# Values as the stationary operand in column halves, scores two pairs ahead, and the output half per token tile

## The chip, the core and the metric

The kernel runs on one core of a Trainium2 chip. What counts is the device time of one execution in microseconds, as the median over runs. TensorE is written PE (its weight loads PEld), VectorE DVE, ScalarE ACT, GpSimd POOL, SyncE SP.

## The reference, cut to what matters

All arithmetic is float32, one sequence of 256 tokens, width 1024. Two first-block layers hold a mixer, a cross attention to a memory of 256 rows, and a gated convolution network. Two second-block layers hold a gated network, a mixer and another gated network. The parts that the change touches are the attentions:

```python
# first mixer: 8 heads of neighbourhood attention (all 4 rows of keys are seen here,
# with a bias and a column mask) and 8 query heads over 2 key heads; head size 64
p = softmax(scores); o = p @ v
out = concat([na_out, gqa_out], -1) @ w_out
# memory block: 4 heads of size 128; second mixer: 16 heads of size 64, causal;
# and beside it the state-space part:
xdt   = silu(xs) * dt
cb    = C_chunk @ B_chunk.T
y     = (cb * lmat) @ xdt + carry(chunk 0 -> chunk 1) + d_skip * silu(xs)
```

## The kernel before, in words

Activations are held transposed, features on partitions, as two fp32r parts, high and low (`Features`), and every weight matrix product is three fp32r matmuls (`mm3`, L256). A weight unit of 128x2048 comes by two DMAs on SP's queue (`wunit`, L234); ACT copies it to `hi`, DVE subtracts to `lo`, with three buffers of each. Such a product costs 3 matmuls of 256 or 512 moving columns per feature tile.

Attention works in pairs of heads (`Pair`, L414) for one token tile of 128 queries. `S` multiplies queries (stationary) with keys; heads of size 64 lie in the two row halves of the array, and two pairs (mates) share one S step. On DVE and ACT `softmax` (L532) takes the row maximum, then exp with the row sum as a by-product (`den`). `T` transposes the unnormalised probabilities on PE (2 transposes of 128x128 per head with 256 keys) and ACT copies them to SBUF (`pts`). `V` multiplies: stationary the transposed probabilities (128 keys by 128 queries), moving the values of a head (64 columns; 128 in the memory block), so that a bank `po` collects [queries, 8 heads x 64]. All these are plain float32 matmuls, which stand as two records each in the trace; transposes stand as one. At the end of a group (8 heads, or 4 in the memory block) `divide` (L477) multiplies `po` by the reciprocal of `den` into SBUF, and `turn` (L484) transposes it back with four transposes; `split` (L401) writes the two parts of the result.

`pipeline` (L495) sets the order by hand: at step i it issues S of pair i+look, T of pair i, V of pair i-1, and `turn` two steps after a group's end; one step more and the group's key is in `done`. After each of these it yields, and `weave` (L161) issues filler steps at a rate. PE's order is exactly this order; for the other engines a planner orders by the text and by when operands are ready. In the first mixer the filler (L710) is `values()` (16 steps of one `mm3`), then, once token tile 1 of the grouped heads is done, `half_g()` (L691: the output projection of the grouped half, both token tiles, 16 steps), then the first quarter of `half_n()`. It starts with three steps owed at rate 1.0 and look=1. The memory block and the second mixer have look=2; the latter's filler is `conv()`.

`ssd()` (L1128) is the state-space part, woven with the projection of the gate. Its text: silu of xs, the two `xdt` products, `xd0` (chunk 0 times its decay), two `d_skip` products, four `cb` products with their masks, then eight rounds: `decay()` of the next round (L1149: DVE makes `ar`, PE sums it into `sg`, ACT takes exp, DVE multiplies by the masked `cb`), `across()` in rounds 0 and 1 (the carry between chunks, which needs `xd0` and `xs`), and the products `y`.

Of the kernel before, what the change touches and what calls it, by code (L numbers as in the profile page):

```python
# [16 lines left out]
P = 128  # L17
# [95 lines left out]
def unit(a, spec):  # L113

    kind, name, l, r0, c0 = spec
    if kind == "G":
        (ng, nv), (cg, cv) = name, c0
        both = np.stack([a[ng][l][:, cg : cg + P], a[nv][l][:, cv : cv + P]], 1)
        return both.reshape(KD, P, 2 * P).transpose(1, 0, 2).reshape(P, 2048)
    w = a[name][l]  # L120
    if kind == "T":
        z = np.zeros((P, 2048), w.dtype)
        z.reshape(P, 2, KD, P)[:, 0, :, :16] = w[:, c0 : c0 + 16].reshape(KD, P, 16).transpose(1, 0, 2)
        return z
    if kind == "W":
        return w[:, c0 : c0 + 256].reshape(8, P, 256).transpose(1, 0, 2).reshape(P, 2048)
    if kind == "M":
        return w[r0 : r0 + 512, c0 : c0 + 512].reshape(4, P, 512).transpose(1, 0, 2).reshape(P, 2048)
    return w[r0 : r0 + 256, :].reshape(2, P, 1024).transpose(1, 0, 2).reshape(P, 2048)

# [7 lines left out]
class Ring:  # L138


    N = {"w1": (8, 256), "w2": (7, 640), "rb": (2, 256)}

    def __init__(self, pool):
        self.pool = pool
# [31 lines left out]
def two_blocks(ctx: ExitStack, tc: tile.TileContext, specs, x, mem, wall, pf, rowb, fin, rpb, cst, out):  # L176
# [237 lines left out]
    class Pair:  # L414


        def __init__(self, hs, pos, st, nm, n, kts, scores, soft, v, vcol, w):
            self.__dict__.update(hs=hs, pos=pos, st=st, nm=nm, n=n, kts=kts, scores=scores, soft=soft, v=v, vcol=vcol, w=w, end=None, mate=None, beside=None)

        def S(self):  # L420
            n = self.n
            if self.mate is None:
                p = ps(f"s_{self.nm}")
                at = [p[:, b * n : (b + 1) * n] for b in range(2)]
                for b in range(2):
                    self.scores(at[b], b)
                self.pr = [self.soft(at[b], b) for b in range(2)]
            elif self.mate is not True:

                both = (self, self.mate)  # L430
                p = [ps(f"s{b}_{self.nm}") for b in range(2)]
                for j, x in enumerate(both):
                    for b in range(2):
                        x.scores(p[b][:, j * n : (j + 1) * n], b)
                for j, x in enumerate(both):
                    x.pr = [x.soft(p[b][:, j * n : (j + 1) * n], b) for b in range(2)]

        def T(self):
            p = ps(f"pt_{self.nm}")
# [7 lines left out]
        def V(self):  # L447
            st, w, n = self.st, self.w, self.n
            if "po" not in st:
                st["po"] = ps(f"po_{self.nm}")  # L450
            for b in range(2):
                o = st["po"][:, self.pos[b] * w : (self.pos[b] + 1) * w]
                for kt in range(self.kts):
                    T.matmul(o, self.pt[:, b * n + kt * P : b * n + (kt + 1) * P], self.v[:, kt, self.vcol(b) : self.vcol(b) + w],
                             start=kt == 0, stop=kt == self.kts - 1)

    def attention(nm, nheads, tts, mixT, base, group, keys, scores, soft, v, vcol, apart=1, fours=True):

# [2 lines left out]
        pairs = []  # L461
        for tt in tts:
            for g0 in range(0, nheads, group):
                st = {"den": sm.tile([P, 8], F32, tag="den", name=f"den_{nm}{tt}{g0}")}
                firsts = [i for i in range(group) if (i // apart) % 2 == 0]
                for n_, a in enumerate(firsts):
                    pos = (a, a + apart)
                    hs = (g0 + a, g0 + a + apart)
                    pairs.append(Pair(
                        hs, pos, st, f"{nm}{tt}_{g0 + a}", keys(tt), keys(tt) // P,  # L470
                        lambda o, b, hs=hs, tt=tt: scores(o, hs[b], tt),
                        lambda s, b, hs=hs, tt=tt, st=st, pos=pos: soft(s, hs[b], tt, st["den"][:, pos[b] : pos[b] + 1], f"{nm}{tt}_{hs[b]}"),
                        v, lambda b, hs=hs: vcol(hs[b]), w))
                    if fours and n_ % 2:
                        pairs[-2].mate, pairs[-1].mate = pairs[-1], True

                def divide(st=st, tt=tt, g0=g0):  # L477
                    rd = sm.tile([P, 8], F32, tag="rd", name=f"rd_{nm}{tt}{g0}")
                    V.reciprocal(rd[:, :group], st["den"][:, :group])
                    st["o"] = wk.tile([P, 512], F32, tag="w2", name=f"o_{nm}{tt}{g0}")  # L480
                    V.tensor_tensor(st["o"].rearrange("p (h d) -> p h d", h=group), st["po"].rearrange("p (h d) -> p h d", h=group),
                                    bl(rd[:, :group], w), ALU.mult)

                def turn(st=st, tt=tt, g0=g0):  # L484
                    p = ps(f"ot_{nm}{tt}{g0}")
                    for i in range(4):
                        T.transpose(p[:, i * P : (i + 1) * P], st["o"][:, i * P : (i + 1) * P], ident)
                    split(mixT.four(base + g0 * w // 512, tt), p.rearrange("p (a b) -> p a b", a=4))

                pairs[-1].end = (divide, turn, (nm, tt, g0))  # L490
        return pairs

    done = set()
# [1 line left out]
    def pipeline(pairs, look=1, before_v=None, drain=5, lag=2):  # L495
        pend = []
        n = len(pairs)
        for i in range(-look, n + 1):
# [10 lines left out]
            if i >= 1:  # L509
                pairs[i - 1].V()  # L510
                if pairs[i - 1].end:
                    pairs[i - 1].end[0]()
                    pend.append((i + lag, pairs[i - 1].end[1]))
                    pend.append((i + lag + 1, lambda k=pairs[i - 1].end[2]: done.add(k)))
                yield
            while pend and pend[0][0] <= i:
                pend.pop(0)[1]()
# [29 lines left out]
    def mixer1(l, nrm, nx):  # L547
# [140 lines left out]
                       lambda s, h, tt, den, nm: softmax(s, na_bias(h, tt), den, nm), nv, lambda h: h * 64)  # L688


        def half_g():  # L691
            for c in range(2):
                p = [ps(f"wg{l}{c}{tt}") for tt in range(2)]
                yield from gen_M("w_out", l, 512, c * 512, list(enumerate(p)), mixT, 4, 4)
                for tt in range(2):
                    residual(tt, c, p[tt])

        units = []

# [7 lines left out]
                    yield  # L707
            residual(tt, c, p)

        fill = chain(values(), after((f"gq{l}", 1, 0), half_g()), after((f"na{l}", 0, 0), half_n(0, 0)))  # L710
        weave(pipeline(gqa + na, drain=4), fill, 1.0, 3)
        run(fill)
        run(half_n(0, 1))
        run(half_n(1, 0))
# [196 lines left out]
    def mixer2(l, nrm, nx):  # L911
# [216 lines left out]
        def ssd():  # L1128
# [2 lines left out]
            late.pop(0)()  # L1131
            for tt in range(2):
                A.activation(xs[:, tt, :], xs[:, tt, :], AF.Silu)
            for tt in range(2):
                V.tensor_tensor(h16(xdt[:, tt, :]), h16(xs[:, tt, :]), bl(dt[:, tt * 16 : (tt + 1) * 16], 64), ALU.mult)
            V.tensor_tensor(h16(xd0), h16(xdt[:, 0, :]), bl(dec[:, 0:16], 64), ALU.mult)
            for tt in (1, 0):
                V.tensor_tensor(h16(xs[:, tt, :]), h16(xs[:, tt, :]), bl(rbc("d_skip_2", l), 64), ALU.mult)

            for g in range(4):  # L1140
                p = ps(f"cb{nm}{g}")
# [27 lines left out]

            todo = [(g, c) for g in range(4) for c in range(2)]  # L1170
            lms = {todo[0]: decay(*todo[0])}
            yield
            yp = {}
            for i, (g, c) in enumerate(todo):
                if i + 1 < len(todo):
                    lms[todo[i + 1]] = decay(*todo[i + 1])
                    yield
                if i < 2:
                    across(i)
                yield  # L1180
                q = g // 2
                if (c, q) not in yp:
# [136 lines left out]
```

## Time and profile before

| | us |
|---|---|
| median of 3 runs | 1973.94 |
| lowest and highest | 1973.42, 1974.88 |
| profiled execution | 1978.73 |
| its span (first to last instruction) | 1976.9 |
| mean granted PE clock in it | 0.993 |

The busy time of PE counts each matmul to its modelled end; matmuls overlap, so the busy time of a group is not the sum of what its members cost. What one costs in a stream is the distance from its start to the next start. The granted clock is 1.00 at 2.4 GHz and 0.50 at 1.2 GHz.

### The profile page before, as it was taken

Reading aid. Unit: us, or ns where it says so; the run is one execution under the profiler, and the core shown is the slowest. Engines: PE = TensorE matmul, PEld = TensorE weight load, DVE = VectorE, ACT = ScalarE, POOL = GpSimd, SP = SyncE. Lnnn points to the kernel's source line nnn. Section 1 sums busy time; section 2 is a strip of 40 time slices with the busy share of each in tenths; the row PEclk is TensorE's granted clock in tenths of the full one; section 3 lists DMA queues with packets and bytes.
Section 4 is the critical chain, followed back from the end, with each engine's and each line's share of the span. In section 5 each row is a group of like instructions: output and inputs, shape, how many; then the busy total and the mean of one; then the engine's idle time right before and its main releaser. Section 6 shows DMA issues by size and latency. Waiting matters only on the chain.

```text
span 1976.9 us, 33687 instructions
## 1 busy us (share of the span) xinstructions
PE 1954.4 (99%) x13082; PEld 1787.3 (90%) x13082; DVE 1405.1 (71%) x3065; ACT 1057.8 (54%) x1801; POOL 7.6 (0%) x108
## 2 busy tenths in 40 slices
PE   8999999999999999999999999999999999999999
PEld 7788999887999999999899789999999889889998
DVE  6666887775778778656868876666655868877564
ACT  5565555655665555444576554445444567555442
POOL 0000000000000000000000000000000000000000
PEclk9899999999999999999999999999999999999999
DMA  7334565552436555555543356555555553355553
GB/s 264 122 108 155 169 200 188 185 182 86 167 124 212 186 187 180 184 190 183 170 157 113 105 161 207 183 185 169 194 191 187 179 169 117 107 161 178 186 183 124
DMA packets 90992, 331.01 MB, mean 167 GB/s; under 512 B 10064, under 2 KB 10576, under 8 KB 90576
## 3 DMA queue, kind: packets, MB, share of 16 engines
q1 hardware_dynamic: 90832, 328.86, 50.6%
q8 instruction: 102, 1.67, 0.3%
q14 instruction: 58, 0.48, 0.1%
HBM read 327.77 MB, written 1.05 MB: 166 GB/s over the span
## 4 chain that ended last, share of the span: by engine, by line
PE 94%; DVE 3%; ACT 1%; DMA 1%; issue 1%; SPq 0%; DVEq 0%; ACTq 0%
PE upffn L259 26%; PE upc L259 13%; PE accffn L259 12%; PE accc L259 6%; PE xbb L259 5%; PE wob L259 4%; PE qkb L259 4%; PE vb L259 2%; PE zb L259 2%; PE gq L259 1%; PE wg L259 1%; PE mk L259 1%; PE mq L259 1%; DMA raw<-in_wall 1%; PE mo L259 1%; PE mv L259 1%
## 5 line engine op out<-in xcount | busy, mean ns | idle before, releaser
L253 DVE TENSOR_TENSOR lo<-raw,hi 128x512 fp32r<-128x512 f32 x1220 | 795.2, 685 | 223.7 <-ACT hi L250 222.2
L250 ACT ACTIVATE hi<-raw 128x1024 fp32r<-128x1024 f32 (+1 forms) x611 | 628.3, 1052 | 594.1 <-issue 365.9
L259 PE MATMUL upffn<-hT_s,hi 128*128 128x256 f32 x2816 | 509.5, 283 | 0.0
L259 PEld LDWEIGHTS upffn<-hT_s,hi 128*128 128x128 f32 x2816 | 441.7, 192 | 3.0
L259 PE MATMUL upffn<-hT_s,lo 128*128 128x256 f32 x1408 | 398.4, 283 | 0.0
L259 PEld LDWEIGHTS upffn<-hT_s,lo 128*128 128x128 f32 x1408 | 270.1, 192 | 0.0
L259 PE MATMUL upc<-hT_f,hi 128*128 128x256 f32 x1408 | 254.9, 283 | 0.0
L259 PE MATMUL accffn<-hi,mix_fffn 128*128 128x512 f32 x704 | 223.8, 390 | 0.0
L259 PEld LDWEIGHTS upc<-hT_f,hi 128*128 128x128 f32 x1408 | 220.9, 192 | 1.6
L259 PE MATMUL upc<-hT_f,lo 128*128 128x256 f32 x704 | 199.2, 283 | 0.0
L259 PEld LDWEIGHTS accffn<-hi,mix_fffn 128*128 128x128 f32 x704 | 132.3, 188 | 26.7
L901 DVE TENSOR_TENSOR u_ffn<-upffn,rb_s 128x512 f32<-128x512 f32 x80 | 55.2, 690 | 126.6 <-PE upffn L259 126.6
L259 PE MATMUL accffn<-lo,mix_fffn 128*128 128x512 f32 x352 | 137.4, 390 | 0.0
L259 PEld LDWEIGHTS upc<-hT_f,lo 128*128 128x128 f32 x704 | 135.0, 192 | 0.0
L259 PE MATMUL accc<-hi,mix_fc 128*128 128x512 f32 x352 | 112.1, 390 | 0.0
L259 PE MATMUL xbb<-hT_b,hi 128*128 128x256 f32 x512 | 103.3, 297 | 0.0
L259 PEld LDWEIGHTS xbb<-hT_b,hi 128*128 128x128 f32 x512 | 78.3, 190 | 3.6 <-issue 2.6
L259 PE MATMUL qkb<-hi,hT_b 128*128 128x512 f32 x256 | 81.0, 393 | 0.0
L259 PEld LDWEIGHTS accc<-hi,mix_fc 128*128 128x128 f32 x352 | 66.2, 188 | 13.3
L259 PEld LDWEIGHTS accffn<-lo,mix_fffn 128*128 128x128 f32 x352 | 66.2, 188 | 12.2
L259 PE MATMUL xbb<-hT_b,lo 128*128 128x256 f32 x256 | 72.1, 282 | 0.0
L259 PE MATMUL accc<-lo,mix_fc 128*128 128x512 f32 x176 | 68.7, 390 | 0.0
(403 smaller groups left out, 3001.6 us busy)
## 6 DMA issues: line engine op xcount, KB each, us to landing
raw<-in_wall SPq DMA_DIRECT2D x609, 512.0 KB, 4.2
TB<-in_rpb SPq DMA_DIRECT2D x2, 1536.0 KB, 9.5
MEM<-in_mem SPq DMA_DIRECT2D x2, 1024.0 KB, 4.9
x_in<-in_x SPq DMA_DIRECT2D x4, 256.0 KB, 5.5
out<-x_in SPq DMA_DIRECT2D x4, 256.0 KB, 2.0
C<-in_cst SPq DMA_DIRECT2D x1, 544.0 KB, 9.3
raw<-in_wall SPq DMA_DIRECT2D x2, 256.0 KB, 6.8
FIN<-in_fin SPq DMA_DIRECT2D x1, 512.0 KB, 7.6
```

Of the source, the lines that this page charges most:

```text
L250: A.activation(hi[:, q], raw[:, i : i + n], AF.Copy)
L253: V.tensor_tensor(lo[:, q], raw[:, i : i + LOW], hi[:, q].bitcast(F32), ALU.subtract)
L259: T.matmul(o, st[a], mv[b], start=first and i == 0, stop=last and i == 2)
L901: V.tensor_tensor(u, p, b2(rb), ALU.mult)
```

## The change

`V` swaps the operands: the values of a head are stationary (128 keys by 64 columns) and the transposed probabilities are moving (128 queries). The two heads of a pair write the two partition halves of `po`, that is the two column halves of the array, in turn over the key tiles. `po` so holds the transposed output; `turn` goes, and `split` reads `po` at once. Since the rows are now features, the division moves ahead of the transposes: after the softmax each pair gets a reciprocal and one multiplication per head on the probabilities, in SBUF. For the grouped heads (pairs of head a and a+4) the rows of `w_out` are laid out on the host to fit. The first mixer's pipeline looks two pairs ahead, its filler runs at rate 0.8 with nothing owed, and `half_g` runs per token tile, with its two weight units kept from the first token tile to the second. The ring of 256-wide work tiles has 14 buffers instead of 8. In `ssd()` only the first `xdt` product stands at the beginning; the second follows the first `decay()`, `xd0` and the first `d_skip` the second `decay()`, the other `d_skip` the third, and `across()` moves to rounds 2 and 4.

```diff
+        if name == "w_out" and r0 == 512:
+            w, r0 = w[512:].reshape(2, 4, 64, -1).transpose(1, 0, 2, 3).reshape(512, -1), 0
...
-    N = {"w1": (8, 256), "w2": (7, 640), "rb": (2, 256)}
+    N = {"w1": (14, 256), "w2": (7, 640), "rb": (2, 256)}
...
                 self.pr = [self.soft(at[b], b) for b in range(2)]
+                self.divide()
...
                     x.pr = [x.soft(p[b][:, j * n : (j + 1) * n], b) for b in range(2)]
+                    x.divide()
+        def divide(self):
+            rd = sm.tile([P, 2], F32, tag="rd", name=f"rd_{self.nm}", bufs=4)
+            V.reciprocal(rd, self.den)
+            for b in range(2):
+                V.tensor_scalar(self.pr[b][:, : self.n], self.pr[b][:, : self.n], rd[:, b : b + 1], None, ALU.mult)
...
-            for b in range(2):
-                o = st["po"][:, self.pos[b] * w : (self.pos[b] + 1) * w]
-                for kt in range(self.kts):
-                    T.matmul(o, self.pt[:, b * n + kt * P : b * n + (kt + 1) * P], self.v[:, kt, self.vcol(b) : self.vcol(b) + w],
-                             start=kt == 0, stop=kt == self.kts - 1)
+            both = [(b, kt) for b in range(2) for kt in range(self.kts)]
+            if w == 64:
+                both.sort(key=lambda x: x[1])
+            for b, kt in both:
+                r, c = (rows[b], self.at) if w == 64 else (slice(0, P), self.at + b)
+                T.matmul(st["po"][r, c * P : (c + 1) * P], self.v[:, kt, self.vcol(b) : self.vcol(b) + w],
+                         self.pt[:, b * n + kt * P : b * n + (kt + 1) * P], start=kt == 0, stop=kt == self.kts - 1)
...
-                def divide(st=st, tt=tt, g0=g0):
-                    rd = sm.tile([P, 8], F32, tag="rd", name=f"rd_{nm}{tt}{g0}")
-                    V.reciprocal(rd[:, :group], st["den"][:, :group])
-                    st["o"] = wk.tile([P, 512], F32, tag="w2", name=f"o_{nm}{tt}{g0}")
-                    V.tensor_tensor(st["o"].rearrange("p (h d) -> p h d", h=group), st["po"].rearrange("p (h d) -> p h d", h=group),
-                                    bl(rd[:, :group], w), ALU.mult)
-                def turn(st=st, tt=tt, g0=g0):
-                    p = ps(f"ot_{nm}{tt}{g0}")
-                    for i in range(4):
-                        T.transpose(p[:, i * P : (i + 1) * P], st["o"][:, i * P : (i + 1) * P], ident)
-                    split(mixT.four(base + g0 * w // 512, tt), p.rearrange("p (a b) -> p a b", a=4))
-                pairs[-1].end = (divide, turn, (nm, tt, g0))
+                def put(st=st, tt=tt, g0=g0):
+                    split(mixT.four(base + g0 * w // 512, tt), st["po"].rearrange("p (a b) -> p a b", a=4))
+                pairs[-1].end = (put, (nm, tt, g0))
...
-                    pend.append((i + lag, pairs[i - 1].end[1]))
-                    pend.append((i + lag + 1, lambda k=pairs[i - 1].end[2]: done.add(k)))
+                    pend.append((i + lag, lambda k=pairs[i - 1].end[1]: done.add(k)))
...
-        def half_g():
+        units_g = []
+        def half_g(tt):
             for c in range(2):
-                p = [ps(f"wg{l}{c}{tt}") for tt in range(2)]
-                yield from gen_M("w_out", l, 512, c * 512, list(enumerate(p)), mixT, 4, 4)
-                for tt in range(2):
-                    residual(tt, c, p[tt])
+                p = ps(f"wg{l}{c}{tt}")
+                if tt == 0:
+                    units_g.append(wunit("M", "w_out", l, 512, c * 512))
+                for k in range(4):
+                    mm3(p, mixT.k(4 + k, tt), cut(units_g[c], k * 512, (k + 1) * 512), k == 0, k == 3)
+                    yield
+                residual(tt, c, p)
...
-        fill = chain(values(), after((f"gq{l}", 1, 0), half_g()), after((f"na{l}", 0, 0), half_n(0, 0)))
-        weave(pipeline(gqa + na, drain=4), fill, 1.0, 3)
+        fill = chain(values(), after((f"gq{l}", 0, 0), half_g(0)), after((f"gq{l}", 1, 0), half_g(1)),
+                     after((f"na{l}", 0, 0), half_n(0, 0)))
+        weave(pipeline(gqa + na, 2, drain=4), fill, 0.8)
...
-            for tt in range(2):
+            def times_dt(tt):
                 V.tensor_tensor(h16(xdt[:, tt, :]), h16(xs[:, tt, :]), bl(dt[:, tt * 16 : (tt + 1) * 16], 64), ALU.mult)
-            V.tensor_tensor(h16(xd0), h16(xdt[:, 0, :]), bl(dec[:, 0:16], 64), ALU.mult)
-            for tt in (1, 0):
+            def times_d(tt):
                 V.tensor_tensor(h16(xs[:, tt, :]), h16(xs[:, tt, :]), bl(rbc("d_skip_2", l), 64), ALU.mult)
+            times_dt(0)
...
             lms = {todo[0]: decay(*todo[0])}
+            times_dt(1)
             yield
             yp = {}
             for i, (g, c) in enumerate(todo):
                 if i + 1 < len(todo):
                     lms[todo[i + 1]] = decay(*todo[i + 1])
                     yield
+                if i == 0:
+                    V.tensor_tensor(h16(xd0), h16(xdt[:, 0, :]), bl(dec[:, 0:16], 64), ALU.mult)
                 if i < 2:
-                    across(i)
+                    times_d(i)
+                if i in (2, 4):
+                    across(i // 2 - 1)
```

## Rows read from the trace of the kernel before

**Rows 1.** The page, part 1: busy us, share of the span, instructions.

```profile
PE 1954.4 (99%) x13082; PEld 1787.3 (90%) x13082; DVE 1405.1 (71%) x3065; ACT 1057.8 (54%) x1801; POOL 7.6 (0%) x108
```

**Rows 2.** Stretches of core 0: length, busy time by engine, granted clock, DMA.

```profile
75.09:100.12 25.03, 23.74 (x138) 19.38 (x136) 11.29 (x38) 15.30 (x44) 0.00 (x0) 0.73 0.15 45
442.83:463.85 21.02, 19.17 (x138) 15.35 (x136) 10.78 (x37) 14.02 (x40) 0.00 (x0) 0.92 0.17 51
1006.36:1079.76 73.40, 73.40 (x626) 70.47 (x625) 59.66 (x178) 53.23 (x126) 0.63 (x6) 1.00 0.35 113
1093.71:1103.66 9.95, 6.65 (x16) 5.05 (x16) 7.37 (x15) 4.39 (x7) 0.00 (x0) 0.66 0.16 53
1709.22:1718.07 8.85, 5.51 (x16) 4.07 (x16) 7.37 (x15) 4.39 (x7) 0.00 (x0) 0.81 0.19 60
```

**Rows 3.** Waits of TensorE: us in total, times, longest.

```profile
PE sgb L1154 <- DVE ar_b L1153: 6.6, 2, 3.3
```

**Rows 4.** Timeline of TensorE, first mixer: start, length to the modelled end, instructions.

```profile
69.80 1.13 PE L673 MATMUL s_gq<-G,qm 64*128 64x256 f32 x8
70.87 0.50 PE L259 MATMUL nav<-hi,hT_a 128*128 128x512 f32 x1
...
71.69 0.60 PE L443 MATMUL pt_gq<-C,pr_gq 128*128 128x128 f32 x4
72.04 0.48 PE L259 MATMUL nav<-hi,hT_a 128*128 128x512 f32 x1
...
72.82 1.00 PE L454 MATMUL po_gq<-G,pts_gq 128*128 128x64 f32 x8
73.64 0.48 PE L259 MATMUL nav<-hi,hT_a 128*128 128x512 f32 x1
```

**Rows 5.** Timeline of TensorE, ssd() of layer 0, full clock.

```profile
1105.26 0.62 PE L1154 MATMUL sgb<-ar_b,gtr 128*128 128x512 f32 x2
...
1108.66 1.00 PE L1186 MATMUL yb<-xdt_b,lm_b 128*128 128x64 f32 x8
```

**Rows 6.** Timeline of TensorE: second block's scores and products, memory block's products.

```profile
1011.06 0.40 PE L259 MATMUL xbb<-hT_b,hi 128*128 128x256 f32 x2
1011.30 0.28 PE L259 MATMUL xbb<-hT_b,lo 128*128 128x256 f32 x1
1011.51 0.71 PE L1020 MATMUL s_db<-kT_b,qm 64*128 64x128 f32 x8
1012.15 0.50 PE L259 MATMUL xbb<-hT_b,hi 128*128 128x256 f32 x2
...
1015.55 0.56 PE L454 MATMUL po_db<-v_b,pts_db 128*128 128x64 f32 x4
1015.92 0.48 PE L259 MATMUL xbb<-hT_b,hi 128*128 128x256 f32 x2
...
178.18 1.06 PE L454 MATMUL po_me<-M,pts_me 128*128 128x128 f32 x8
179.02 0.50 PE L259 MATMUL mo<-hi,mix_m 128*128 128x512 f32 x1
```

**Rows 7.** Groups of DVE by form: count, busy us, mean ns of one.

```profile
L481 DVE TENSOR_TENSOR o_db<-po_db,rd_db 128x512 f32<-128x512 f32 x8 | 5.5, 684 | 2.1 <-PE po_db L454 2.1
...
L345 DVE TENSOR_SCALAR dg_s<-C,y_s 128x128 f32<-128x128 f32 x8 | 1.9, 284 | 0.1
...
L479 DVE RECIPROCAL rd_me<-den_me 128x4 f32<-128x4 f32 x4 | 0.7, 168 | 0.0
```

**Rows 8.** Timeline of TensorE, first transposes of layer 0; idle time in brackets.

```profile
60.19 0.90 PE L443 MATMUL pt_gq<-C,pr_gq 128*128 128x128 f32 x4 [0.66 <-ACT pr_gq L539]
```

**Rows 9.** Timeline of DVE before the second decay().

```profile
1089.27 2.35 DVE L1135 TENSOR_TENSOR xdt_b<-xs_b,dt_b 128x1024 f32<-128x1024 f32 x2
1091.54 1.21 DVE L1136 TENSOR_TENSOR xs_b<-xdt_b,dec_b 128x1024 f32<-128x1024 f32 x1
1092.68 2.34 DVE L1138 TENSOR_TENSOR xs_b<-xs_b,RBt 128x1024 f32<-128x1024 f32 x2
```

More of the change, by code (lines that the diff above doesn't have):

```diff
@@ L414, in two_blocks, with __init__ @@
     class Pair:
-        def __init__(self, hs, pos, st, nm, n, kts, scores, soft, v, vcol, w):
-            self.__dict__.update(hs=hs, pos=pos, st=st, nm=nm, n=n, kts=kts, scores=scores, soft=soft, v=v, vcol=vcol, w=w, end=None, mate=None, beside=None)
+        def __init__(self, hs, at, st, nm, n, kts, scores, soft, v, vcol, w):
+            self.__dict__.update(hs=hs, at=at, st=st, nm=nm, n=n, kts=kts, scores=scores, soft=soft, v=v, vcol=vcol, w=w, end=None, mate=None, beside=None)
         def S(self):
@@ L463, in attention @@
             for g0 in range(0, nheads, group):
-                st = {"den": sm.tile([P, 8], F32, tag="den", name=f"den_{nm}{tt}{g0}")}
+                st = {}
                 firsts = [i for i in range(group) if (i // apart) % 2 == 0]
                 for n_, a in enumerate(firsts):
-                    pos = (a, a + apart)
                     hs = (g0 + a, g0 + a + apart)
+                    den = sm.tile([P, 2], F32, tag="den", name=f"den_{nm}{tt}{g0}{a}", bufs=4)
                     pairs.append(Pair(
-                        hs, pos, st, f"{nm}{tt}_{g0 + a}", keys(tt), keys(tt) // P,
+                        hs, n_ if w == 64 else a, st, f"{nm}{tt}_{g0 + a}", keys(tt), keys(tt) // P,
                         lambda o, b, hs=hs, tt=tt: scores(o, hs[b], tt),
-                        lambda s, b, hs=hs, tt=tt, st=st, pos=pos: soft(s, hs[b], tt, st["den"][:, pos[b] : pos[b] + 1], f"{nm}{tt}_{hs[b]}"),
+                        lambda s, b, hs=hs, tt=tt, den=den: soft(s, hs[b], tt, den[:, b : b + 1], f"{nm}{tt}_{hs[b]}"),
                         v, lambda b, hs=hs: vcol(hs[b]), w))
+                    pairs[-1].den = den
                     if fours and n_ % 2:
                         pairs[-2].mate, pairs[-1].mate = pairs[-1], True
-                def divide(st=st, tt=tt, g0=g0):
-                    rd = sm.tile([P, 8], F32, tag="rd", name=f"rd_{nm}{tt}{g0}")
-                    V.reciprocal(rd[:, :group], st["den"][:, :group])
-                    st["o"] = wk.tile([P, 512], F32, tag="w2", name=f"o_{nm}{tt}{g0}")
-                    V.tensor_tensor(st["o"].rearrange("p (h d) -> p h d", h=group), st["po"].rearrange("p (h d) -> p h d", h=group),
-                                    bl(rd[:, :group], w), ALU.mult)
-                def turn(st=st, tt=tt, g0=g0):
-                    p = ps(f"ot_{nm}{tt}{g0}")
-                    for i in range(4):
-                        T.transpose(p[:, i * P : (i + 1) * P], st["o"][:, i * P : (i + 1) * P], ident)
-                    split(mixT.four(base + g0 * w // 512, tt), p.rearrange("p (a b) -> p a b", a=4))
-                pairs[-1].end = (divide, turn, (nm, tt, g0))
+                def put(st=st, tt=tt, g0=g0):
+                    split(mixT.four(base + g0 * w // 512, tt), st["po"].rearrange("p (a b) -> p a b", a=4))
+                pairs[-1].end = (put, (nm, tt, g0))
         return pairs
```

## The prediction

> **What bounds the kernel now.** I read the page first: TensorE is busy 99% of the span [rows 1], so on the average there is nothing to fill. That average hides its own gaps, because the ends of matmuls are modelled and a matmul at the half clock counts as busy. So I went on to the busy time by stretches [rows 2], the waits of TensorE [rows 3] and the timeline, in which the distance from one start to the next start is the true price. There the reader is to see three places:
>
> 1. First block's mixer, from the last step of values() to the first of half_g(): no filler is left, and attention runs alone, for 25.03 us in layer 0 and 21.02 us in layer 1, with a mean granted clock of 0.73 and 0.92 [rows 2]. By the loop L495 a stretch holds 8 T, 8 V, 4 S and 2 turn() of 4 records, 8, 8 and 4: 32+64+32+8 = 136, against 138 in the row. At the prices among filler [rows 4], T 72.04-71.69 = 0.35, V 73.64-72.82 = 0.82, S 70.87-69.80 = 1.07, turn() like T: 2.80+6.56+4.28+0.70 = 14.34 us. So 10.69 and 6.68 us are lost, 17.4 in both layers, in waits on the chain S, max, exp, T, copy, V, and in the fall from the 2.4 to the 1.2 GHz level that follows.
> 2. Start of ssd(): TensorE waits 3.3 us per layer for ar, the input of the second decay() [rows 3], and then falls to 1.2 GHz. From the end of the matmul before the wait to the first y products 9.95 and 8.85 us pass [rows 2]; the same sequence of instructions takes 1108.66-1105.26 = 3.40 at full clock [rows 5]. Lost: 6.55+5.45 = 12.0 us.
> 3. Everywhere else around the change TensorE is dense: second block's attention, 73.40 us of layer 0, has TensorE busy throughout and DVE 59.66, 81% [rows 2].
>
> **The change part by part.**
>
> *Transposes of the output.* turn() goes: 20 groups (per layer 2+2+2+4) of four transposes on a bound engine, 20 x 0.35 [rows 4] = **-7.0**. The copy and subtraction that split the result stay, now straight from the products' bank.
>
> *Products with values stationary.* The trace has no column half. Now four matmuls of 64 moving columns cost 0.82 (48 pairs), two cost 1015.92-1015.55 = 0.37 (16 pairs, second block's first token tile) [rows 4, 6]. Afterwards the moving side has 128 columns and the array is used in halves. The nearest row is scores in row halves with the same count and width: four matmuls of 128 columns, 1012.15-1011.51 = 0.64, plus 0.09 in which they start late (1011.30 to 1011.51 is 0.21, the matmuls just before are 0.12 apart) = 0.73 [rows 6]. The 256-column scores take 1.07 without the late start [rows 4], so 4x128 columns are worth 1.07-0.64 = 0.43 and entering and leaving the half mode 0.73-0.43 = 0.30. Hence 0.73 against 0.82 in 48 pairs, and 0.30+0.43/2 = 0.52 against 0.37 in 16: -4.3+2.4 = **-1.9**. Ends: with no overlap of the halves each matmul costs what a full one of 128 columns does, (179.02-178.18)/4 = 0.21 [rows 6], so 0.84+0.30 = 1.14 and 0.72: +15.4+5.6 = +21. With full overlap and free switching, half of today: 48 x 0.41 + 16 x 0.185 = -22.6. I take the row halves, the only half mode that the trace shows. The memory block (width 128) keeps full-array products of the same size: 0.
>
> *Division before the transposes.* Each of 72 pairs gets on DVE a reciprocal, 0.17, and two multiplications. A 128x128 tensor_scalar takes 0.28, a 128x512 PSUM-to-SBUF product 0.68 [rows 7]; 128x256 lies between, 0.42 interpolated. So 1.01 us per pair of 256 keys, 0.73 per pair of 128; 0.68+0.17 per group goes. It lies in the chain between exp and T. First block's mixer: T comes two pairs after its S, with two T, two V, another S and about four filler steps between (0.70+1.46+1.07+4x0.78 = 6.3 us by [rows 4, 6]); the 1.0 that the chain grows by hides there, and if that cover were gone it is 1 us a pair. At the start it is not hidden: T of the first pair already waits 0.66 [rows 8]; now it comes after two filler steps and a second S (1.56+1.07) instead of five steps (3.9 at 72.82-72.04 = 0.78 each [rows 4]), about 1 us earlier, and its input is 1 us later: 2 us per layer. Second block: per layer 8x0.73+8x1.01-4x0.85 = 10.5 us more DVE in the 73.40 us, 59.66+10.5 = 70.2, about 97% of what is left of it. That much load must show somewhere; between 0 and all of it (21 for both layers) I take **+4**. Memory block: its last T has no filler ahead, +1 per layer, **+2** (0 to 4).
>
> *Filler per token tile, scores two ahead, rate 0.8.* Counting yields of the new loop: values() (16 steps plus the closing one) lasts to the 22nd yield instead of the 13th; the key of token tile 0 is set at the 23rd; its eight steps reach to the 32nd; token tile 1's key comes at the 36th, so three or four yields have no filler; its eight steps reach the 45th of 56. The dry stretch all but goes. I give back the 2 us at the start and 0.5 for the few dry yields per layer: 17.4-5.0 = **-12.4** (0 to -17.4). No matmul is added, the steps are the same 16. The weight units keep their order on SP's queue, and POOL's is not touched; two of three hi/lo buffers are now held until token tile 1 is done, and the next unit but one, which waits for the first of them, is needed some 15 yields later. Were that cover gone, one unit's four subtractions of 0.68 [rows 7] would stand open. The longer w1 ring costs no time.
>
> *ssd().* In DVE's queue five 1024-wide products stand ahead of the second decay(): two xdt 2.35, xd0 1.21, two d_skip 2.34 = 5.90 [rows 9]. After the change xd0 and the d_skip ones (3.55) come behind it, and the wait was 3.3, so it goes almost wholly. Next is the third decay(): xd0 and one d_skip (2.4) now stand ahead of it, with only about one step's slack; I leave 1.5 per layer. across() moves two steps later, its reader at the fourth y is still behind it. 12.0-3.0 = **-9.0** (-3 to -12).
>
> Sum: -7.0-1.9+4+2-12.4-9.0 = **-24.3 us**. The profiled execution took 1978.73 (span 1976.9 and 1.8 around it), so 1954.4 there; it lies 4.8 above the median 1973.94, from which I take the same difference: 1949.6, **1950**. A measurement here tells 0.2%, 4 us, from no change.
>
> **The rivals.**
>
> *A. Halves don't overlap.* Then the products cost +21 instead of -1.9: 1972.5. For it: no row shows a column half. Against: row halves do overlap (0.73 for four matmuls, where full ones take 0.84 without any switching). The Trainium skill (TensorE: Matmul & The Clock Gate, Part 3, The mechanism) says that weight loads overlap running matmuls only where the row group differs, and column halves share their rows; the trace does not bear that out for the full array, whose matmuls follow each other 0.12 apart on the same rows [rows 6]. Chance 0.10.
>
> *B. Products at half price.* -22.6 instead of -1.9: 1929. Against: the late start and the long visit of the row halves. The Trainium skill (TensorEngine Tiling, When to Use Tiling) recommends just this swap for 64 moving columns with a factor of two. Chance 0.07.
>
> *C. DVE bounds second block.* All 21 us of new DVE work show, +17 over the forecast: 1967. For it: 97%; against: DVE's subtractions run a unit ahead and can slip. Chance 0.14.
>
> *D. Divisions exposed, slower.* If the queue order puts each division where T already waits, 32 mixer pairs of the first block cost 32x1.01 and those of the second 16x0.73+16x1.01, together 60 us in place of the 4+4 counted: 1949.6+52 = 2002. Place: T, waiting for pr on DVE; it turns the sign when over about half of that 60 is exposed (24.3+8 = 32). For it: DVE has 97%; against: two pairs of look-ahead. Chance 0.06.
>
> *E. Filler still runs dry* (it waits for keys, or the late start eats it): the -12.4 is missing, 1962. Chance 0.11.
>
> **How the numbers follow.** Forecast 0.52, its own range 1940 to 1960 (ssd and filler by +-5 each, DVE by 6). A 0.10, B 0.07, C 0.14, D 0.06, E 0.11. 1934 to 1970 holds the forecast, E and C, some 0.77, and an edge of B: 0.8. Faster (under 1970): forecast, B, E and most of C, 0.82; A and the rest of C are within 0.2%, 0.11; D and the worst of A slower, 0.07.
>
> **What would show it.** Right: attention of the first mixer without a stretch of TensorE below full clock, no ot rows, TensorE's wait for ar under 1 us and no half clock in ssd, products from start to next start near 0.7 us in 128x64 form. Wrong: products above 1.1 (A) or near 0.4 (B); T of second block waiting for DVE (C, D), with DVE over 95% there; a new dry stretch (E).

## The result and the profile after

The changed kernel takes 1951.43 us (median of 4 runs, 1949.37 to 1952.6) against 1974.41 for the kernel before (1973.42 to 1974.94): ratio 0.9886, 95% interval 0.9872 to 0.99, or -23.0 us. The forecast was 1950, its range 1934 to 1970. The total hides two errors of opposite sign, so the stages are worth reading one by one. In the two profiled executions (1978.73 and 1952.6, -26.1), measured from the first matmul of one tile to the first of the next, both layers:

| stage | before | after | difference | predicted |
|---|---|---|---|---|
| first mixer, attention and output projection | 76.81 + 72.36 | 65.43 + 69.76 | -14.0 | -18.1 |
| memory block's attention | 30.94 + 30.94 | 30.88 + 30.88 | -0.1 | +0.6 |
| second block's attention | 73.40 + 73.40 | 71.68 + 71.68 | -3.4 | +2.2 |
| ssd() and what follows up to the next block | 90.80 + 89.70 | 85.77 + 85.78 | -9.0 | -9.0 |

The predicted column is the sum of the prediction's terms, sorted by stage: the first mixer holds the filler's -12.4, eight groups of transposes and 32 pairs of products; the memory block four groups and the +2; the second block eight groups, products of both kinds and DVE's +4.

Page part 1 of the kernel after, to set beside [rows 1]:

```profile
PE 1928.7 (99%) x13002; PEld 1744.2 (89%) x13002; DVE 1431.7 (73%) x3241; ACT 1057.2 (54%) x1801; POOL 7.8 (0%) x108
```

TensorE has 80 instructions less, the 20 groups of four transposes, and none with an ot tile is left. DVE has 27 us more. Stretches of the kernel after (columns as in [rows 2]): the first mixer of both layers, the part of layer 1 at half clock, the second block's attention, and zb to wob, in which ssd() lies:

```profile
54.48:119.91 65.43, 63.39 (x410) 45.34 (x409) 50.33 (x151) 41.41 (x105) 0.00 (x0) 1.00 0.38 124
411.75:481.51 69.76, 65.65 (x409) 47.05 (x409) 47.74 (x138) 43.27 (x106) 0.00 (x0) 0.95 0.35 108
417.92:424.75 6.83, 4.89 (x18) 3.90 (x20) 5.59 (x18) 3.54 (x13) 0.00 (x0) 0.50 0.40 130
992.62:1064.30 71.68, 71.68 (x610) 63.82 (x609) 65.62 (x219) 53.44 (x126) 0.63 (x6) 1.00 0.34 115
1064.30:1098.29 33.99, 33.04 (x167) 27.34 (x166) 31.66 (x55) 18.73 (x28) 0.00 (x0) 1.00 0.36 117
```

The third number from the end of each line is the granted clock. Layer 0's first mixer, which had a stretch at 0.73 [rows 2], is at 1.00 throughout; ssd(), which had 0.66 and 0.81, is at 1.00. One stretch at half clock is new, at the start of layer 1. In the second block TensorE is busy without a gap, with DVE at 65.62 of 71.68, 92%. The waits of TensorE in the kernel after (us in all, times, longest) name the new place:

```profile
PE pt_gq L455 <- DVE pr_gq L448: 6.2, 2, 4.1
PE pt_me L455 <- DVE pr_me L448: 3.1, 2, 1.5
PE sgb L1167 <- DVE ar_b L1166: 1.7, 2, 0.8
```

The wait for ar fell from 3.3 per layer [rows 3] to 0.85. The first transposes of a layer now wait for the division: 2.04 and 4.11, against 0.66 in layer 0 before [rows 8]. Why 4.11 in layer 1 is read in the queues of ScalarE and TensorE there (timeline of the kernel after: start, length, idle time and what ended it in brackets):

```profile
413.72 1.13 PE L677 MATMUL s_gq<-G,qm 64*128 64x256 f32 x8
...
419.86 1.09 PE L455 MATMUL pt_gq<-C,pr_gq 128*128 128x128 f32 x4 [4.11 <-DVE pr_gq L448]
```

```profile
415.07 1.06 ACT L253 ACTIVATE hi<-raw 128x1024 fp32r<-128x1024 f32 x1 [2.22 <-DMA raw<-in_wall]
416.15 1.28 ACT L543 ACT_TABLE_LOAD   x1
417.44 0.47 ACT L543 ACTIVATE pr_gq<-s_gq,nmx_gq 128x256 f32<-128x256 f32 x1
```

The scores started at 411.75, but the first exp only at 417.44: ahead of it in ScalarE's queue stands the split of a weight unit that waits 2.22 us for its transfer, and then a table load. TensorE has two filler steps to offer, and waits from 415.75 to 419.86. The granted clock falls within that wait, at 417.92, and stands at 0.50 for the 6.83 us above, 4.89 of them behind the wait. Which layer waits how long differs from one execution to the next: e1 and e12 below, whose start is that of the kernel after, show 3.19 and 2.13, and 2.54 and 2.06.

The price of a product visit (the products of one pair between other work), timeline of the kernel after:

```profile
67.14 0.40 PE L262 MATMUL nav<-hi,hT_a 128*128 128x512 f32 x1
67.46 0.66 PE L468 MATMUL po_gq<-pts_gq,G 128*64 128x128 f32 x8
68.05 0.50 PE L262 MATMUL nav<-hi,hT_a 128*128 128x512 f32 x1
...
109.68 1.09 PE L468 MATMUL po_na<-pts_na,A 128*64 128x128 f32 x16
110.70 0.50 PE L262 MATMUL wn<-hi,mix_a 128*128 128x512 f32 x1
...
1015.26 0.44 PE L468 MATMUL po_db<-pts_db,v_b 128*64 128x128 f32 x4
1015.63 0.50 PE L262 MATMUL xbb<-hT_b,hi 128*128 128x256 f32 x2
```

Four products take 68.05-67.46 = 0.59 and start 0.09 late (0.32 behind the matmul before them, where 0.23 is usual), 0.68 in all (0.73 predicted, 0.82 before [rows 4]); eight in one visit 1.02, so four more cost 0.43 and the visit itself 0.25. Two take 0.37+0.09 = 0.46 (0.52 predicted, 0.37 before [rows 6]).

### The profile page after: what moved, and what is told of

The parts are those of the page before. It is cut to its first block, busy times and chain, and to the rows that moved or that the text cites. A ratio compares the mean times of both kernels' runs of the same rounds, so it can differ in the third digit from the quotient of the medians.

```text
span 1950.8 us, 33631 instructions
## 1 busy us (share of the span) xinstructions
PE 1928.7 (99%) x13002; PEld 1744.2 (89%) x13002; DVE 1431.7 (73%) x3241; ACT 1057.2 (54%) x1801; POOL 7.8 (0%) x108
## 4 chain that ended last, share of the span: by engine, by line
PE 93%; DVE 4%; DMA 1%; ACT 1%; issue 1%; SPq 0%; ACTq 0%; DVEq 0%
PE upffn L262 26%; PE accffn L262 12%; PE upc L262 12%; PE accc L262 6%; PE xbb L262 5%; PE wob L262 5%; PE qkb L262 4%; PE vb L262 2%; DMA raw<-in_wall 1%; PE wg L262 1%; PE gq L262 1%; PE nav L262 1%; PE mk L262 1%; PE mq L262 1%; PE wn L262 1%; PE mo L262 1%
## 5 line engine op out<-in xcount | busy, mean ns | idle before, releaser
L262 PEld LDWEIGHTS accffn<-lo,mix_fffn 128*128 128x128 f32 x352 | 66.2, 188 | 12.2
```

Of the source, the lines that this page charges most:

```text
L262: T.matmul(o, st[a], mv[b], start=first and i == 0, stop=last and i == 2)
```

## The experiments

Times are medians, with the ratio to the kernel before and its 95% interval. The kernel before had medians of 1973.72 (e1 to e4), 1973.07 (e5 to e8) and 1974.09 (e9 to e12).

### ssd() alone: e3

The kernel before with the function ssd() of the kernel after.

> The kernel before with the new order in ssd() alone. Theory queue order: the wait of 3.3 us per layer for the second decay and the half clock behind it go by themselves: -9 us, 1965.4, the wait for ar under 2 us in all, nothing else moves. Rival relief: the wait goes only with the multiplications and buffers that the new attention gives free ahead of ssd(): under -4, above 1970.

Measured 1963.81 (0.9951, 0.9936 to 0.9966), -9.9; zb to wob went from 39.87 and 38.77 to 33.96 and 33.97. The term held. Its profile holds one thing more: the first mixer, whose code is that of before, took 73.78 and 72.50 us instead of 76.81 and 72.36. That is taken up below.

### The price of the products: e1 and e12

e1 takes the alternation of the two column halves away:

```
-            if w == 64:
-                both.sort(key=lambda x: x[1])
```

> The changed kernel with the two heads' products one after the other instead of in turn. Theory overlap: two column halves run at the same time only when neighbours lie in different halves, so the 48 visits of four products go from 0.68 to about 1.0 us (two or three of the four no longer overlap, 0.1 each), 48 x 0.3 = +14: about 1965 us. Rival short load: the gain is the weight load of 64 instead of 128 columns; then a visit stays at 0.68 and the time at 1951 within 1.

Measured 1952.43 (0.989, 0.9875 to 0.9904). A visit takes 0.60 (69.62 to 70.22), as with alternation, and the time is within the 1 us that the rival "short load" asked for. The order of the halves, from which I had expected overlap, buys nothing.

e12 loads 128 columns of values, in the full array (the order is that of e1):

```
-                r, c = (rows[b], self.at) if w == 64 else (slice(0, P), self.at + b)
-                T.matmul(..., self.v[:, kt, self.vcol(b) : self.vcol(b) + w], ...)
+                r, c = (slice(0, P), self.at + (0 if w == 64 else b))
+                v0 = self.vcol(0 if w == 64 else b)
+                T.matmul(..., self.v[:, kt, v0 : v0 + P], ...)
```

> The kernel after with 128 columns of values held stationary where it has 64 (the neighbour's columns beside the own ones), written over all 128 rows of the bank, without the alternation of halves: the same number of products with the same 128 moving columns, in full-array form; the second head of a pair overwrites what the first one wrote, so the attention outputs of the mixers are left wrong. Theory (the price of these products is that of loading the stationary side, and 64 columns load in half the time): a visit of four costs what the memory block's 128x128 products cost, about 0.82 to 0.84 against 0.68 from start to start with its late start, 48 visits, and two cost 0.42 against 0.46: +6 over the kernel after (+3 to +9), 1954 to 1960. Rival (the price goes by the moving columns, and the half form is what costs 0.25 a visit): 0.43 a visit, 0.25 less in 64 visits, 1935 to 1940.

Measured 1953.95 (0.9895, 0.9875 to 0.9914). In the total that is 2.5 over the kernel after, just below the range I gave. The rows show both sides of it. Timeline of e12:

```profile
75.60 0.40 PE L262 MATMUL nav<-hi,hT_a 128*128 128x512 f32 x1
75.84 1.05 PE L467 MATMUL po_gq<-pts_gq,G 128*128 128x128 f32 x8
76.65 0.47 PE L262 MATMUL nav<-hi,hT_a 128*128 128x512 f32 x1
```

The visit takes 0.81, and starts on time (0.24 after the matmul before it): 0.81 against 0.68 with a late start. Summed over the stage, start to next start, the products take 13.5 and 13.3 us instead of 9.25 and 9.45. The rival, which wanted 0.43 a visit, fell. The first mixer as a whole moved by +4.4 and -2.0, because layer 1 did not wait long at its start this time; the second block stayed at 71.69 in both, where I had expected some +0.8 per layer: there the products cost 1.83 more, start to next start, and what stands around them, starting on time, 1.82 less. So: with 128 moving columns, four products cost 0.81 with 128 stationary columns in the full array and 0.43 with 64 in column halves, and the half form costs 0.25 a visit. The moving columns are not what sets the 0.81, for the products of the kernel before, with 64 of them, took 0.82 [rows 4]. The weight load PEld (tile po_gq, shortest, median and longest in ns; the kernel after, then e12) is shorter with 64 columns:

```profile
L468 PEld LDWEIGHTS po_gq<-pts_gq,G x128: 132/137/231, 62.9 to 450.0; 128*64 128x64 f32 x128
L467 PEld LDWEIGHTS po_gq<-pts_gq,G x128: 187/192/338, 63.3 to 449.7; 128*128 128x128 f32 x128
```

That fits. But e12 changes the columns and the form (halves to full array) together, so that the load sets the price is argued, not shown; and the scores, with 128 stationary columns in row halves, take only 0.64 for four [rows 6], so the count of columns alone is no rule for every form.

### Does the division cost: e5

Two more multiplications of the same size, by a constant, behind each division:

```
                 V.tensor_scalar(self.pr[b][:, : self.n], self.pr[b][:, : self.n], rd[:, b : b + 1], None, ALU.mult)
+                V.tensor_scalar(self.pr[b][:, : self.n], self.pr[b][:, : self.n], 1.0, None, ALU.mult)
```

> The kernel after, with each pair's two divisions followed by two multiplications by 1.0 of the same size on DVE (0.70 us more per pair of 256 keys, 0.56 per pair of 128, 72 pairs, 48 us in all, in the chain from exp to the transposes). Theory: the look-ahead of two pairs hides the division wherever attention is under way, and only the two starts of the first mixer show it, 0.7 each, and the start and end of the memory block, 0.7 each; in second block DVE goes from 65.6 of 71.68 us to 65.6+10.1 = 75.7, so there, and only there, it becomes the bound: up to +4 per layer. In all +3 to +12 over the kernel after, 1954 to 1963, with the first mixer's steady part unchanged. Rival (divisions exposed): each pair pays its 0.6 to 0.7, +40 to +48, about 1995, and then the divisions of the kernel after cost some 60 us as well. Rival (DVE has room even so): second block's stages stay at 71.7, 1952 to 1954.

Measured 1953.57 (0.9895, 0.9866 to 0.9923), +2.1. The second block of e5:

```profile
993.14:1064.82 71.68, 71.68 (x611) 63.82 (x609) 68.25 (x248) 53.32 (x126) 0.63 (x6) 1.00 0.32 109
```

DVE is busy for 68.25 of 71.68, 95%, and the stage is not a hundredth longer. I had DVE at 75.7 here, counting the single duration of a division's multiplication, 0.35 and 0.28; the added ones, by a constant, last 0.29 and 0.22, and the next instruction starts before the one ahead of it has ended (timeline under *Division* below). Some of the load also moved out of the stage: 32 added instructions would give x251, and x248 are there; a weight subtraction and the two halves of ar, 0.68 each, are no longer in it, and behind it zb to wob takes 34.13 and 34.15 instead of 33.99. The rival "DVE has room" held, and that the division is exposed pair by pair fell. What shows besides is +0.47 per layer in the memory block; the waits at the start, 2.88 and 2.51, lie within those of kernels without the added work (2.04 and 4.11 in the kernel after).

### The start: e2 and e8

e2 has three filler steps owed when attention starts, as before had; e8 five:

```
-        weave(pipeline(gqa + na, 2, drain=4), fill, 0.8)
+        weave(pipeline(gqa + na, 2, drain=4), fill, 0.8, 3)
```

> The changed kernel with three filler steps owed at the start of the first mixer, as the kernel before had. Theory start wait: the first transposes wait 2.0 and 4.1 us for probabilities; three more steps of 0.70 ahead of them take 2.1 us off each, and the half clock behind the second wait goes; the filler runs dry three yields sooner, which costs under 1 us a layer: 1945 to 1948 us. Rival conservation: the steps are missing later and cost there what they gain here: 1951 within 1.5.

Measured 1945.59 (0.9856, 0.9841 to 0.9871), the fastest kernel of this study, 5.8 under the kernel after, as the theory had it. First mixer of e2, both layers:

```profile
54.10:120.26 66.16, 63.20 (x410) 45.52 (x409) 51.19 (x153) 41.45 (x105) 0.00 (x0) 1.00 0.38 126
411.56:474.90 63.34, 63.09 (x409) 45.52 (x409) 46.81 (x138) 43.00 (x106) 0.00 (x0) 1.00 0.35 118
```

Layer 1 is free of waits but for 0.25 and takes 63.34; that is what the stage costs when nothing is missing.

> The kernel after, with five filler steps owed at the start of the weave instead of none (the earlier run with three took 1945.6 and left a wait of 1.3 us for pr and 1.7 for pts in layer 0). Theory (the start is a plain wait for the chain of the first pair): two more steps, 1.56 us, cover the rest of layer 0's, and the steps are missing nowhere else: 1943 to 1945. Rival (steps taken early are missing later): a short dry stretch between values() and the key of token tile 0, where values() now ends six yields sooner: 1946 to 1951, with a wait of TensorE in the middle of the stage.

Measured 1948.91 (0.9869, 0.9844 to 0.9895). Layer 1 took 64.12, layer 0 69.60, with a wait of 2.86 before the first products, during which the clock falls to 0.50 for 6.83 us (in the profiled execution, 1949.77; the fastest of the four, at a mean clock of 1.000, took 1946.04). The time lies in the rival's range, but that wait is neither theory's. Timeline of ScalarE and DVE in e8:

```profile
64.71 0.47 ACT L543 ACTIVATE pr_gq<-s_gq,nmx_gq 128x256 f32<-128x256 f32 x1 [3.62 <-DVE nmx_gq L542]
...
62.46 1.89 DVE L256 TENSOR_TENSOR lo<-raw,hi 128x512 fp32r<-128x512 f32 x3
64.27 0.74 DVE L542 TENSOR_REDUCE nmx_gq<-s_gq 128x1 f32<-128x256 f32 x2
```

Steps taken earlier bring the next weight unit's subtractions earlier into DVE's queue, here three of them (1.89) ahead of the maximum of a later pair, where e2 has one (0.69); that pair's exp waits for the maximum 3.62 us on ScalarE, and behind that exp stands the copy of the transposes on which the first products wait.

### Filler per token tile, look-ahead, rate: e4, e6, e7, e9, e10, e11

e4 is the kernel before with this part alone (half_g for one token tile, two pairs ahead, 0.8 steps per yield, the longer w1 ring).

> The kernel before with the first mixer's new filler, rate, look-ahead and ring alone; products, transposes and division as before. Theory filler: the dry stretches of 25 and 21 us go without the new products, and the start waits less than in the changed kernel as no division stands there: first mixer -13 to -16 us in both layers together, 1959 to 1962. Rival products: the stretch got short because turn() and dear products left it; then under -8 here, above 1966.

Measured 1968.67 (0.9972, 0.9961 to 0.9984), -5.05: a miss; the total lies where the rival "products" had it, whose reason e10 below tests. No stretch of the first mixer is below full clock any more, so the mechanism works; the size does not. Where the time of layer 0 went, start to next start by tile, before and e4: scores 10.4 and 8.5, transposes 10.1 and 7.4, products 16.9 and 13.5, turn() 2.2 and 1.6, together -8.6; but values() 13.0 and 14.2, half_g() 12.2 and 12.95, half_n() 11.2 and 11.3, together +2.1, from the wait at the start and because each return from attention to filler costs something: behind four transposes the first filler matmul takes 88.53-88.21 = 0.32 to the next start, where 0.23 is usual. In layer 1: -5.0 and +3.4.

Which of its three parts does it? In the kernel after, e6 takes up half_g() for both token tiles late, as before; e7 goes back to one pair ahead; e9 does both. (Of e6's edit only the order of the filler is shown; half_g() itself is again that of before.)

```
-        fill = chain(values(), after((f"gq{l}", 0, 0), half_g(0)), after((f"gq{l}", 1, 0), half_g(1)),
+        fill = chain(values(), after((f"gq{l}", 1, 0), half_g()),
```

```
-        weave(pipeline(gqa + na, 2, drain=4), fill, 0.8)
+        weave(pipeline(gqa + na, 1, drain=4), fill, 0.8)
```

> The kernel after, with the gqa half of the output projection taken up for both token tiles only after the second one's key, as in the kernel before; look-ahead, rate, products and division are those of after. Theory (the filler of token tile 0 is what fills the dry stretch): with 0.8 steps per yield values() is used up at about yield 22 and the next filler comes at yield 36, so some 14 yields, six pairs, run dry again and TensorE falls to its 1.2 GHz level: +6 to +14, 1958 to 1965, with half clock in both layers. Rival (a look-ahead of two pairs lets attention run dense without filler): within 3 us of after. Rival (filler per tile costs by breaking up TensorE's modes): faster than after by 1 to 3 us.

Measured 1951.3 (0.9884, 0.9859 to 0.9909): no loss at all. My theory fell, the rival held. A dry stretch is there, but short, and two pairs ahead keep it nearly dense:

```profile
80.04:89.21 9.17, 8.08 (x77) 5.49 (x75) 7.20 (x29) 9.17 (x25) 0.00 (x0) 1.00 0.16 57
```

In these 9.17 us of e6 TensorE waits twice, 0.65 and 0.44, and the granted clock stays at 1.00. The even total hides a small price. In the profiled execution layer 0 takes 66.61, 1.2 more than in the kernel after, and layer 1 67.10, 2.7 less, because its start waited 1.59 and 0.90 this time instead of 4.11 and kept its clock. e11 below, with three steps owed in front, shows the price.

> The kernel after, with scores one pair ahead in the first block's mixer instead of two. From its scores to its transposes a pair needs 4.4 us in the trace of after (5.7 less the 1.28 of a table load); with one pair ahead about one V, one other S and 2.4 filler steps, 0.68+1.07+1.9 = 3.7 us, stand between. Theory (the second pair ahead is what hides the division): about 0.7 per pair is exposed, 32 pairs, and some clock with it: +10 to +35, 1961 to 1986; the start itself gets shorter by one S. Rival (one pair ahead is enough, as in the kernel before): within 4 us of after.

Measured 1957.62 (0.9915, 0.9891 to 0.9939), +6.2, in neither range. The excess is at the start (waits for pr of 3.50 and 4.01, each with 6.83 us at half clock, in which the filler behind it is slow too); past it no wait of the mixer is over 0.21. With filler, one pair ahead does carry the division, against what I had expected.

> The kernel after with scores one pair ahead and with the gqa half of the output projection taken up only after the second token tile's key: the fourth cell beside after (both edits, 1951.4), late filler with two pairs ahead (1951.3) and filler per tile with one pair ahead (1957.6). Theory (either edit by itself is enough to keep attention dense, and the one covers what the other would): without both, some six pairs run alone, each waiting for its chain of 4.4 us behind about 2 us of other work, and the clock falls: 10 to 20 us above the last of the three, 1967 to 1977, half clock in both layers. Rival (the rate of 0.8, which stretches values() over more pairs, does it): within 3 us of 1957.6, and no half clock in the middle of the stage.

Measured 1968.7 (0.9977, 0.9966 to 0.9988), 11.1 above e7 and 17.4 above e6, as the theory had it. The dry stretch is back, with waits and half clock (the scores take 95.25-93.24 = 2.01 instead of 1.07), timeline of e9:

```profile
91.14 1.12 PE L455 MATMUL pt_na<-C,pr_na 128*128 128x128 f32 x4 [2.79 <-DVE pr_na L448]
92.19 1.12 PE L468 MATMUL po_gq<-pts_gq,G 128*64 128x128 f32 x8
93.24 2.08 PE L681 MATMUL s_na<-A,qm 64*128 64x256 f32 x8
95.25 1.11 PE L455 MATMUL pt_na<-C,pr_na 128*128 128x128 f32 x4
```

So in the steady part filler per tile and the second pair ahead each cover most of what the other does: with both 1951.4, without the first 1951.3, without the second 1957.6 (the excess at the start), without either 1968.7. The rate of 0.8, which all four have, does not do it by itself.

e10 puts the whole old schedule into the kernel after (weave(pipeline(gqa + na, 1, drain=4), fill, 1.0, 3), late half_g); e11 is e6 with three steps owed.

> The kernel after (products in column halves, division before the transposes, new order of ssd) with the whole schedule of the first block's mixer from the kernel before: one pair ahead, late filler, one step per yield, three steps owed. Theory (the schedule carried about as much as the dry stretch had lost, and the earlier division makes one pair ahead worse): the dry stretch is back over some ten pairs, 17 us as before and 1 us per pair for the division in the chain, less about 6 for a shorter start: 1962 to 1975. Rival (the new products, without turn(), are what made attention dense): 1946 to 1952.

Measured 1958.17 (0.9917, 0.9897 to 0.9937), 6.7 above the kernel after, below my range: waits for pr of 2.08, 1.21 and 1.29 in layer 0's dry stretch, but the half clock only at the start of layer 0 and for a few us of layer 1. The rival fell too, as those waits show, and with it the reason of e4's rival: the new products by themselves leave the dry stretch with more waits than before, not fewer (in layer 0 before, past the start, 0.17 and 1.01).

> The kernel after with two pairs ahead and 0.8 steps per yield as it has them, but late filler (both token tiles after the second key) and three steps owed at the start. Theory (the start is a wait of its own, worth 6 us, and late filler costs nothing with two pairs ahead): the 1951.3 of late filler alone less about 6, 1943 to 1947, level with the 1945.6 of three steps owed with filler per tile. Rival (three steps taken early lengthen the dry stretch from about six pairs to nine, long enough for the clock to fall): 1950 to 1956, with half clock in the middle of the stage.

Measured 1948.3 (0.987, 0.9847 to 0.9893): stages of 66.38 and 65.32, no half clock, but 1.7 us of waits for pr_na in a dry stretch that is now longer. Between the two theories; the start is worth 3 here, and filler per tile the other 2.7 to e2. So late filler does cost something with two pairs ahead.

## Why the prediction was right, and where only its sum was

The kernel before, e3, e10 and after differ by one group of edits each, so the sum can be set against what was measured:

| step | predicted | measured |
|---|---|---|
| ssd() | -9.0 | -9.9 (e3) |
| products, turn(), division away from the start | -7.0-1.9+4+2 = -2.9 | -5.6 (e3 to e10) |
| filler, look-ahead, rate, with the start | -12.4 | -6.7 (e10 to after); -5.05 (e4, in the old code) |

*ssd().* Right in place, size and remainder: 0.85 us of wait is left per layer, 1.5 was kept back.

*Transposes and products.* The 20 groups went at their price. Of the products the price was near (0.68 and 0.46 for 0.73 and 0.52), its reason was not, so that was in part luck: I read it from row halves that overlap. e1 shows that the order of the column halves does nothing, and e12 that full-array products with 128 stationary columns cost nearly twice as much. Rival A therefore didn't come, though no run shows the overlap that I had argued against it. Rival B's half price is true of the products themselves (0.43 against 0.82 before), and 0.25 per visit takes more than half of that gain back. The Trainium skill (TensorEngine Tiling, When to Use Tiling) gives the factor of two; the trace agrees inside a visit, and the visit itself, for which that section has no price, is on top.

*Division.* The +4 for DVE in the second block didn't come. The step that failed is "that much load must show somewhere": DVE rose by 65.62-59.66 = 6.0 per layer, not 10.5, since two multiplications of 128x256 in a row take 0.52 from start to next start and not 0.84 (timeline of e8; the kernel after has the same):

```profile
60.41 0.60 DVE L448 TENSOR_SCALAR pr_gq<-pr_gq,rd_gq 128x256 f32<-128x256 f32 x2
60.93 0.55 DVE L664 TENSOR_TENSOR TB<-TB,C 128x384 f32<-128x384 f32 x1
```

And e5 raises DVE to 95% of the stage at no more than the 0.15 that show behind it. Rivals C and D fell. The memory block's +2 was met by what the transposes gave back there (-0.1 in all).

*The filler.* This is the term that was wrong by half, for three reasons. First its price was taken from the slowest rows: 17.4 us were lost in the dry stretches of one execution, which lay 4.8 above the median. e3's profile shows the same code 2.9 us shorter over both layers, with 13.7 us at half clock instead of 17.1, and still lies 2.4 above e3's median, at a mean granted clock of 0.996 against 0.999 to 1.000 in e3's other runs; and among the runs of the kernel before that were timed beside the experiments the four with a mean granted clock of 0.993 took 1978.0 to 1981.7, the two with 0.998 1971.85 and 1969.88. So the surplus, as far as these runs show it, lay in the very stretch that the change removes, and yet I also took it off the total. Secondly I had the filler steps at no cost, as "the same 16"; among attention they are dearer, in e4 by 0.9 per layer in the two output projections (12.94 and 11.32 against 12.24 and 11.15), in part by the returns from attention. With the start made nearly equal (e10 to e2: three steps owed in both, waits there of 3.1 and 3.2 over both layers, though e10 has 3.4 us at half clock behind its first one) the schedule is worth 12.6, where my terms without the start make 16.4. Thirdly the start costs 5.8 (after to e2), where I kept back 4. By the profiles 2.9 of that are waits (6.15 against 3.21 over both layers); the half clock behind the longer wait, which the sum left out, makes some 2.4 more, an estimate from the 4.89 us at half speed. The chain of the first pair holds a split that waits for its transfer, and in layer 1 a table load.

*Its mechanism.* I put the gain down to filler per token tile. As long as two pairs are ahead that edit by itself is worth little in this kernel, nothing by e6 and 2.7 by e11, and e9 shows that it is worth 11 where one is. The diff has two remedies for one loss, and the sum credited the loss to one of them. Rival E, "filler still dry", would for the same reason have cost at most some 3, had the rest come as forecast.

The errors, +5.7 on the filler, -2.7 on products and division and -0.9 on ssd(), leave some 2 of 23 us. That 1950 came so near is in part luck: the forecast looks better than its parts are. Left open: the 0.09 late start of a half visit was measured, not explained; whether the columns or the form halve the price of the products is not shown; and layer 0 of e2 still takes 2.8 more than layer 1, with waits of 1.3 for pr and 1.7 for pts, which e8 could not remove.

## What to carry to other kernels

When a profiled execution lies above the median, find the stretch that holds the surplus before carrying it over: if the change removes that stretch, the surplus goes with it and isn't to be subtracted again. Where two edits cure the same loss, price the loss once and test each edit without the other; and when a schedule is changed in its steady part, count anew what covers the first item, which has no predecessor and whose chain holds what others find done (here 5.8 us, won back by three filler steps up front).

## What was not expected of the hardware

- Four f32 products with 128 moving columns: 0.81 with 128 stationary columns in the full array, 0.43 with 64 in column halves; alternating column halves changes nothing (0.60 against 0.59).
- A visit to the half form costs 0.25 beyond its products, 0.09 of it before the first one starts.
- DVE at 95% of a stage in which TensorE has no gap lengthened it by nothing (71.68 in both); three of its instructions moved behind the stage, which took 0.15 more there.
- In the kernel after the wait of 2.04 us at the start of layer 0 left the granted clock at 1.00; in the one of 4.11 in layer 1 it fell to 0.50 for 6.83 us. In e1 one of 2.13 was followed by 3.41 us at 0.50.
